# How six pairs of activations cross from FF1 to FF2: as split parts, or whole and split on arrival

## The chip, the core and the metric

The kernel runs on one NeuronCore of a Trainium2 chip. Its engines work beside each other, each with an in-order instruction stream of its own: TensorE (PE in the profile; PEld is its weight load), VectorE (DVE), ScalarE (ACT), GpSimd (POOL) and SyncE (SP), which issues most of the DMAs. The metric is the device time of one launch in microseconds, as a median of runs.

## What is computed

One inference step of a one-layer hybrid encoder, for 512 prompt tokens and 128 decode tokens, 640 in all. The change touches only the last part, the feed-forward network:

```python
def merge_and_ffn(x, oa, ob, norm_grp_a, norm_grp_b, w_out, norm_ffn, w_gate, w_up, w_down):
    o = jnp.concatenate([rmsnorm(oa, norm_grp_a), rmsnorm(ob, norm_grp_b)], axis=-1)
    x = x + o @ w_out
    h = rmsnorm(x, norm_ffn)
    return x + (jax.nn.silu(h @ w_gate) * (h @ w_up)) @ w_down
```

The model width is 2048 and the hidden width 5632, that is 44 blocks of 128, or 22 pairs of blocks. All is float32.

## The kernel before

A float32 product is made from three float32r products: each operand is split into a high part (a ScalarE copy to float32r) and a low part (the operand minus its high part, on VectorE or GpSimd). For weights this is `split` (L195, L196); `mm3` (L204 to L206) issues the three matmuls, 128x128 by 128x320.

The feed-forward network runs as 2x2 block products in Winograd's form: `quartet` (from L890) takes four weight blocks and makes seven products p1, p6, p7, p2, p5, p4, p3, which use left operands 0, 1, 2, 4, 3, 5, 6. Of the weight blocks b11, b12, b21, b22, VectorE makes b12-b22 (L927) and s6 (L929); GpSimd makes b22-s6 (L932) for p5 and b21-s6 (L941) for p4. Blocks and s6 share six tiles W, so a `w_down` load (L914, on SP) waits until an earlier block is given up, and the one into s6's tile waits for L941. The 62 tiles S hold the activations.

FF1 (the loop over `i` in NPAIR) makes one pair of hidden blocks at a time from `w_gate` and `w_up`: 8 weight tiles deep, 24 matmuls a product. Each finished pair leaves as seven left operands. `store_part` writes one of them after each later product: normally split, high part through one of two scratch tiles `half` (L992, L995) and low part (L994, L996), to `act_d`. For the pairs in `raw_pairs`, here 1, 2 and 3, the operand is written whole to `first_d` (L988).

FF2 runs 32 steps of a quartet each over `w_down`. A pair is held for eight successive steps, given by START: pairs 0 to 4 are active in step 0, pairs 1 to 5 in step 1, then five at a time until step 6. With five pairs a product has 15 matmuls. When a pair enters, `fetch` (L958, GpSimd's queue) reads its parts, 320 KB an operand; at the border `free` (called after each product of FF1's last quartet) fetches pairs 1 to 3 whole (L968), 160 KB an operand, and splits them: ScalarE L973, VectorE (pairs 1 and 3) or GpSimd (pair 2) L974. Pairs 0 and 4 come as parts. When a pair of `raw_pairs` is given up in steps 0 to 7, `after` stores its parts (L1074, SP) for its second visit. A new pair's fetch is held back by two products (`fetch_waiting`).

The order on each engine is made by a scheduler when the program is built: it places an instruction when its inputs allow, so a load or a store can stand well ahead of the code around it. Four passes add order by hand; `keep_behind` keeps marked ScalarE instructions behind the unmarked one that is written before them.

Of the kernel before, what the change touches and what calls it, by code (L numbers as in the profile page):

```python
# [41 lines left out]
def f(ap):  # L42
    return ap.bitcast(F32)
# [6 lines left out]
class Net:  # L50
# [104 lines left out]
    def keep_behind(self):  # L155

        info = mybir.DependencyInfo(mybir.DependencyClass.NoSync, mybir.DependencyReason.DATA)
        for k, block in enumerate(self.nc.cur_f.blocks):
            inside = [0] * (len(block.instructions) + 1)
            for a, b in self.behind:  # L160
                if k < len(a):
                    inside[a[k]:b[k]] = [1] * (b[k] - a[k])
            last = None
            for i, ins in enumerate(block.instructions):
                if ins.engine == mybir.EngineType.Activation:
                    if not inside[i]:
                        last = ins
                    elif last is not None:
                        self.tc.add_manual_dep(ins, last.name, info, reason="behind")

    def keep_held(self):

# [127 lines left out]
def build(nc, tc, io, pools):  # L300
# [509 lines left out]
    own_b, acts_b = group_operands(ob_d, g_b, ssq, range(8))  # L810
    n.add("decode", decode_a(1))
    x2_d, act_d = dram("x2_d", (KT, P, TOK)), dram("act_d", (7, P, NPAIR, 2, HT))
    first_d = dram("first_d", (7, P, 3, HT))
    r_a, ssq_a = n.get("S"), n.get("S")
    for m in range(KT):
        ps = n.dense([(io["w_out_b"][m], 8)], acts_b)
# [141 lines left out]
        nc.gpsimd.dma_start(out=r(sh(t, 2, HT)), in_=r(act_d[which, :, j]))  # L958
        lefts[j][which] = t, hl

    raw_pairs = active(0)[1:4]

    def free(which):
        n.put("S", *(h[which][0] for h in hs))
        for j in raw_pairs[::2]:
            k = min(2, raw_pairs[-1] + 1 - j)
            raw = n.get("S")
            dma(out=sh(raw, k, HT), in_=first_d[which, :, j - raw_pairs[0]:j - raw_pairs[0] + k])  # L968
            for a in range(k):
                t = n.get("S")  # L970
                hi, lo = hl = pack(t, HT)
                part = raw[:, a * HT:a * HT + HT]
                nc.scalar.activation(hi, part, AF.Identity)  # L973
                (nc.vector, nc.gpsimd)[a].tensor_tensor(lo, part, f(hi), ALU.subtract)  # L974
                lefts[j + a][which] = t, hl
            n.put("S", raw)
        for j in active(0):
            if j not in raw_pairs:
                fetch(j, which)

    parts = []

    def store_part():

        if parts:
            j, which, src, done = parts.pop(0)
            if j in raw_pairs:
                dma(out=first_d[which, :, j - raw_pairs[0]], in_=src)  # L988
            else:
                at = n.emitted()  # L990
                hi = n.scratch()
                nc.scalar.activation(r(hi), src, AF.Identity)  # L992
                n.behind.append((at, n.emitted()))
                nc.vector.tensor_tensor(r(src), src, hi, ALU.subtract)  # L994
                dma(out=act_d[which, :, j, 0], in_=hi)  # L995
                dma(out=act_d[which, :, j, 1], in_=src)  # L996
            n.put("S", *done)
# [62 lines left out]
    def fetch_waiting(left):  # L1060
        while len(waiting) > left:
            for j, which in waiting.pop(0):
                fetch(j, which)

    def step(t, part="all"):
        now = active(t)
# [3 lines left out]
        def after(which):  # L1070
            gone = [j for j in now if j not in nxt]
            for j in gone:
                if j in raw_pairs and t < 8:
                    dma(out=act_d[which, :, j], in_=sh(lefts[j][which][0], 2, HT))  # L1074
            n.put("S", *(lefts[j][which][0] for j in gone))
            waiting.append([(j, which) for j in nxt if j not in now])
            fetch_waiting(2)
# [11 lines left out]
        for name, bank in quartet(cnt, load, [lefts[j] for j in now], None, after, part):  # L1089
# [20 lines left out]
                add(c21, c21, bank)  # L1110
            elif name == "p3":
                add(c12, c12, bank)
            store_part()
            yield name

    def run(*args):
# [151 lines left out]
```

## Time and profile before

| | us |
|---|---|
| median of 3 runs | 2653.17 (2651.87 to 2653.21) |
| the profiled execution, its own time | 2648.2 |
| its span, first to last instruction | 2646.4 |
| PE busy | 2584.1 (98%) |
| VectorE, ScalarE, GpSimd busy | 1978.9, 1069.3, 662.1 |

PE is busy nearly throughout. Its matmuls are pipelined, so a busy PE still says little; the count of matmuls in a stretch, against the same count in a stretch without waits, tells what was lost there. FF1's last quartet runs from about 2021 us; FF2 follows it to the end. In the tables of stretches, the clock is TensorE's granted clock as a share of its full 2.4 GHz (0.50 is its lower level, 1.2 GHz), and the DMA figure is a busy share of the sixteen DMA engines.

### The profile page before, as it was taken

To read this page: it belongs to the slowest core of one execution; us is meant where nothing else is said; L and a number is where in the kernel's file an instruction comes from. 1 tells how busy PE (TensorE), PEld (TensorE's weight loads), DVE (VectorE), ACT (ScalarE), POOL (GpSimd) and SP (SyncE) were. 2 spreads that over 40 slices of the span, in tenths; PEclk is the share of its full clock that TensorE was granted. 3 is DMA by queue.
4 is the path that set the end of the run, shared out by engine and by line. 5 is a ranking of instruction groups with operands and counts; after the bars stand their busy time and mean duration, and the time that the engine had idled before them with its cause. 6 is when DMAs were issued, how large, how long until landed. Compare 5 with 4: busy or idle time off the path is not lost.

```text
span 2646.4 us, 45166 instructions
## 1 busy us (share of the span) xinstructions
PE 2584.1 (98%) x17565; PEld 2527.2 (95%) x17565; DVE 1978.9 (75%) x3071; ACT 1069.3 (40%) x1732; POOL 662.1 (25%) x577
## 2 busy tenths in 40 slices
PE   8999999999999999999999999999999799999997
PEld 8999998999899999999999999999999799999996
DVE  5665566655866888768888888888887677777797
ACT  5443344444633553333443433433444333333343
POOL 0000000000201203333333233233234432333353
PEclk9999999999999999999999999999999899999998
DMA  5322232434655433333433433433436975665655
GB/s 170 105 70 83 87 101 92 129 116 133 216 186 183 156 127 123 115 106 123 142 130 125 140 130 125 144 132 120 150 128 214 372 201 155 170 184 169 185 155 178
DMA packets 178678, 388.47 MB, mean 147 GB/s; under 512 B 21856, under 2 KB 70496, under 8 KB 178464
## 3 DMA queue, kind: packets, MB, share of 16 engines
q1 hardware_dynamic: 153120, 329.21, 38.5%
q0 software_dynamic: 24192, 55.06, 7.3%
q8 instruction: 138, 2.26, 0.4%
q10 hardware_dynamic: 1152, 1.31, 0.1%
q14 instruction: 76, 0.62, 0.1%
HBM read 301.90 MB, written 82.87 MB: 145 GB/s over the span
## 4 chain that ended last, share of the span: by engine, by line
PE 72%; DVE 5%; DMA 4%; ACT 1%; issue 1%; POOL 0%; SPq 0%; DVEq 0%; ACTq 0%
PE dn L204 15%; PE dn L206 15%; PE dn L205 14%; PE at L204 9%; PE at L206 9%; PE at L205 9%; DVE W L196 2%; DMA W<-w_down 1%; PE at L321 1%; DVE S L951 1%; DMA act_d<-half 1%; DMA S<-cka 0%; DMA S<-first_d 0%; ACT W L195 0%; PE at L402 0%
## 5 line engine op out<-in xcount | busy, mean ns | idle before, releaser
L204 PE MATMUL dn<-S,W 128*128 128x320 f32 x3694 | 1158.3, 314 | 5.0 <-ACT W L195 4.4
L206 PE MATMUL dn<-S,W 128*128 128x320 f32 x3694 | 1145.1, 310 | 12.2 <-DVE W L196 12.2
L205 PE MATMUL dn<-S,W 128*128 128x320 f32 x3694 | 1143.8, 310 | 1.1 <-DVE S L200 0.8
L195 ACT ACTIVATE W<-W 128x1024 fp32r<-128x1024 f32 (+2 forms) x632 | 608.2, 963 | 977.5 <-PE dn L205 542.5
L196 DVE TENSOR_TENSOR W<-W,W 128x1024 fp32r<-128x1024 f32 (+2 forms) x632 | 738.4, 1169 | 91.8 <-ACT W L195 88.3
L204 PEld LDWEIGHTS dn<-S,W 128*128 128x128 f32 x3694 | 695.0, 188 | 17.5 <-ACT W L195 6.1
L206 PEld LDWEIGHTS dn<-S,W 128*128 128x128 f32 x3694 | 694.4, 188 | 17.1 <-DVE W L196 15.9
L205 PEld LDWEIGHTS dn<-S,W 128*128 128x128 f32 x3694 | 694.8, 188 | 3.6 <-DVE S L200 1.0
L204 PE MATMUL at<-S,W 128*128 128x320 f32 x1594 | 494.5, 310 | 7.5 <-ACT W L195 7.5
L206 PE MATMUL at<-S,W 128*128 128x320 f32 x1594 | 495.0, 311 | 4.3 <-DVE W L196 4.3
L205 PE MATMUL at<-S,W 128*128 128x320 f32 x1594 | 493.9, 310 | 0.0
L932 POOL TENSOR_TENSOR W<-W,W 128x1024 f32<-128x1024 f32 (+2 forms) x75 | 159.4, 2126 | 641.9 <-DVE W L196 404.8
L204 PEld LDWEIGHTS at<-S,W 128*128 128x128 f32 x1594 | 300.6, 189 | 8.3 <-ACT W L195 8.3
L206 PEld LDWEIGHTS at<-S,W 128*128 128x128 f32 x1594 | 300.4, 188 | 6.5 <-DVE W L196 6.5
L205 PEld LDWEIGHTS at<-S,W 128*128 128x128 f32 x1594 | 300.5, 189 | 0.0
L951 DVE TENSOR_TENSOR S<-S,dn 128x320 f32<-128x320 f32 x358 | 163.7, 480 | 71.1 <-PE dn L206 71.0
L941 POOL TENSOR_TENSOR W<-W,W 128x1024 f32<-128x1024 f32 (+2 forms) x75 | 162.9, 2173 | 115.0 <-DVE W L196 105.1
L927 DVE TENSOR_TENSOR W<-W,W 128x1024 f32<-128x1024 f32 (+2 forms) x76 | 122.4, 1610 | 70.1 <-DMA W<-w_down 36.5
L951 DVE TENSOR_TENSOR S<-S,at 128x320 f32<-128x320 f32 x262 | 123.2, 480 | 51.4 <-PE at L206 50.5
L958 POOL DMA_DIRECT2D S<-act_d x168 | 91.7, 547 | 185.6 <-PE dn L206 94.5
L929 DVE TENSOR_TENSOR W<-W,W 128x1024 f32<-128x1024 f32 (+2 forms) x76 | 83.4, 1097 | 63.0 <-DMA W<-w_up 34.2
L994 DVE TENSOR_TENSOR S<-S,half 128x320 fp32r<-128x320 f32 x133 | 115.1, 886 | 13.5 <-ACT half L992 11.6
(153 smaller groups left out, 2125.8 us busy)
## 6 DMA issues: line engine op xcount, KB each, us to landing
S<-act_d POOLq DMA_DIRECT2D x168, 320.0 KB, 3.9
W<-w_gate SPq DMA_DIRECT2D x88, 512.0 KB
W<-w_up SPq DMA_DIRECT2D x88, 512.0 KB
W<-w_in SPq DMA_DIRECT2D x66, 512.0 KB
W<-w_down SPq DMA_DIRECT2D x64, 384.0 KB
W<-w_down SPq DMA_DIRECT2D x68, 320.0 KB
act_d<-half SPq DMA_DIRECT2D x133, 160.0 KB
act_d<-S SPq DMA_DIRECT2D x133, 160.0 KB
```

The source lines that it names most:

```text
L195: self.nc.scalar.activation(hi, src, AF.Identity)
L196: self.nc.vector.tensor_tensor(lo, src, f(hi), ALU.subtract)
L204: mm(out, a[0], b[0], start=first, stop=False)
L205: mm(out, a[0], b[1], start=False, stop=False)
L206: mm(out, a[1], b[0], start=False, stop=last)
L927: nc.vector.tensor_tensor(b12[:, w], b12[:, w], b22[:, w], sub)
L929: nc.vector.tensor_tensor(s6[:, w], b11[:, w], b12[:, w], sub)
L932: eng.tensor_tensor(b11[:, w], b22[:, w], s6[:, w], sub)
L941: eng.tensor_tensor(b21[:, w], b21[:, w], s6[:, w], sub)
L951: add = lambda o, a, b: nc.vector.tensor_tensor(o, a, b, ALU.add)
L958: nc.gpsimd.dma_start(out=r(sh(t, 2, HT)), in_=r(act_d[which, :, j]))
L994: nc.vector.tensor_tensor(r(src), src, hi, ALU.subtract)
```

## The change

`raw_pairs` becomes the six pairs 0 to 5 that are active in step 0 or 1. All are written whole in FF1. At the border `free` fetches pairs 0 to 4 whole, two at a time (0 and 1, 2 and 3, 4 alone), with VectorE splitting 0, 2 and 4 and GpSimd 1 and 3. Pair 5 is fetched whole in step 0, and pair 0 once more, whole, at the end of step 24, by the new `fetch_raw`; VectorE splits operands 0, 3 and 6 of these, GpSimd the other four. Pairs 1 to 4 (`one_store`) are stored as parts when given up. Those stores are marked, and `keep_behind` now covers SP too, so they stay behind the SP instruction written before them. `store_part` is not called in steps 0 and 1, so the last pair's parts leave from step 2 on.

```diff
--- before.py
+++ after.py
@@ -160,13 +160,14 @@
             for a, b in self.behind:
                 if k < len(a):
                     inside[a[k]:b[k]] = [1] * (b[k] - a[k])
-            last = None
-            for i, ins in enumerate(block.instructions):
-                if ins.engine == mybir.EngineType.Activation:
-                    if not inside[i]:
-                        last = ins
-                    elif last is not None:
-                        self.tc.add_manual_dep(ins, last.name, info, reason="behind")
+            for engine in (mybir.EngineType.Activation, mybir.EngineType.SP):
+                last = None
+                for i, ins in enumerate(block.instructions):
+                    if ins.engine == engine:
+                        if not inside[i]:
+                            last = ins
+                        elif last is not None:
+                            self.tc.add_manual_dep(ins, last.name, info, reason="behind")
 
     def keep_held(self):
 
@@ -810,7 +811,7 @@
     own_b, acts_b = group_operands(ob_d, g_b, ssq, range(8))
     n.add("decode", decode_a(1))
     x2_d, act_d = dram("x2_d", (KT, P, TOK)), dram("act_d", (7, P, NPAIR, 2, HT))
-    first_d = dram("first_d", (7, P, 3, HT))
+    first_d = dram("first_d", (7, P, 6, HT))
     r_a, ssq_a = n.get("S"), n.get("S")
     for m in range(KT):
         ps = n.dense([(io["w_out_b"][m], 8)], acts_b)
@@ -958,14 +959,29 @@
         nc.gpsimd.dma_start(out=r(sh(t, 2, HT)), in_=r(act_d[which, :, j]))
         lefts[j][which] = t, hl
 
-    raw_pairs = active(0)[1:4]
+    ready = active(0)
+    raw_pairs = active(0) + [j for j in active(1) if j not in ready]
+    one_store = raw_pairs[1:5]
+
+    def fetch_raw(j, which, engine):
+        t, spare = n.get("S"), None
+        if len(n.lists["S"]) > 3:
+            spare = n.get("S")
+        raw = n.scratch() if spare is None else spare[:, :HT]
+        dma(out=raw, in_=first_d[which, :, j])
+        hi, lo = hl = pack(t, HT)
+        nc.scalar.activation(hi, raw, AF.Identity)
+        engine.tensor_tensor(lo, raw, f(hi), ALU.subtract)
+        if spare is not None:
+            n.put("S", spare)
+        lefts[j][which] = t, hl
 
     def free(which):
         n.put("S", *(h[which][0] for h in hs))
-        for j in raw_pairs[::2]:
-            k = min(2, raw_pairs[-1] + 1 - j)
+        for j in ready[::2]:
+            k = min(2, ready[-1] + 1 - j)
             raw = n.get("S")
-            dma(out=sh(raw, k, HT), in_=first_d[which, :, j - raw_pairs[0]:j - raw_pairs[0] + k])
+            dma(out=sh(raw, k, HT), in_=first_d[which, :, j:j + k])
             for a in range(k):
                 t = n.get("S")
                 hi, lo = hl = pack(t, HT)
@@ -974,9 +990,6 @@
                 (nc.vector, nc.gpsimd)[a].tensor_tensor(lo, part, f(hi), ALU.subtract)
                 lefts[j + a][which] = t, hl
             n.put("S", raw)
-        for j in active(0):
-            if j not in raw_pairs:
-                fetch(j, which)
 
     parts = []
 
@@ -985,7 +998,7 @@
         if parts:
             j, which, src, done = parts.pop(0)
             if j in raw_pairs:
-                dma(out=first_d[which, :, j - raw_pairs[0]], in_=src)
+                dma(out=first_d[which, :, j], in_=src)
             else:
                 at = n.emitted()
                 hi = n.scratch()
@@ -1060,7 +1073,10 @@
     def fetch_waiting(left):
         while len(waiting) > left:
             for j, which in waiting.pop(0):
-                fetch(j, which)
+                if j in raw_pairs and j not in one_store:
+                    fetch_raw(j, which, nc.vector if which % 3 == 0 else nc.gpsimd)
+                else:
+                    fetch(j, which)
 
     def step(t, part="all"):
         now = active(t)
@@ -1070,8 +1086,10 @@
         def after(which):
             gone = [j for j in now if j not in nxt]
             for j in gone:
-                if j in raw_pairs and t < 8:
+                if j in one_store and t < 8:
+                    at = n.emitted()
                     dma(out=act_d[which, :, j], in_=sh(lefts[j][which][0], 2, HT))
+                    n.behind.append((at, n.emitted()))
             n.put("S", *(lefts[j][which][0] for j in gone))
             waiting.append([(j, which) for j in nxt if j not in now])
             fetch_waiting(2)
@@ -1110,7 +1128,8 @@
                 add(c21, c21, bank)
             elif name == "p3":
                 add(c12, c12, bank)
-            store_part()
+            if t > 1:
+                store_part()
             yield name
 
     def run(*args):
```

GpSimd at the end of FF1, around b21-s6 of the last quartet (L941, then L942). In the names, S and W are tiles, with a number of the tile and one of its use. Before:

```order
L974 TENSOR_TENSOR S27_3184_21531<-S32_3182_21526,S27_3184_21531 128x320
L958 DMA S40_3187_21539<-act_d_7841 128x640
L1040 TENSOR_TENSOR S8_3152_21296<-S8_3152_21296,S36_1948_11142 128x640
L958 DMA S2_3188_21541<-act_d_7841 128x640
L958 DMA S57_3196_21586<-act_d_7841 128x640
L958 DMA S44_3197_21588<-act_d_7841 128x640
L958 DMA S32_3208_21636<-act_d_7841 128x640
L974 TENSOR_TENSOR S48_3193_21578<-S28_3191_21573,S48_3193_21578 128x320
L941 TENSOR_TENSOR W11_3209_21639<-W11_3209_21639,W1_3179_21496 128x1024
L958 DMA S28_3207_21634<-act_d_7841 128x640
L958 DMA S36_3360_22458<-act_d_7841 128x640
L974 TENSOR_TENSOR S39_3204_21626<-S50_3202_21621,S39_3204_21626 128x320
```

After:

```order
L990 TENSOR_TENSOR S27_3163_21447<-S32_3161_21442,S27_3163_21447 128x320
L1053 TENSOR_TENSOR S8_3131_21212<-S8_3131_21212,S36_1948_11142 128x640
L959 DMA S36_3326_22273<-act_d_7841 128x640
L990 TENSOR_TENSOR S40_3166_21455<-S10_3164_21450,S40_3166_21455 128x320
L942 TENSOR_TENSOR W11_3191_21567<-W11_3191_21567,W1_3158_21412 128x1024
L990 TENSOR_TENSOR S32_3173_21498<-S41_3171_21493,S32_3173_21498 128x320
L990 TENSOR_TENSOR S45_3185_21550<-S12_3183_21545,S45_3185_21550 128x320
L990 TENSOR_TENSOR S57_3176_21506<-S10_3174_21501,S57_3176_21506 128x320
L990 TENSOR_TENSOR S10_3188_21558<-S43_3186_21553,S10_3188_21558 128x320
L990 TENSOR_TENSOR S15_3197_21603<-S23_3195_21598,S15_3197_21603 128x320
L990 TENSOR_TENSOR S37_3200_21611<-S1_3198_21606,S37_3200_21611 128x320
L990 TENSOR_TENSOR S20_3210_21662<-S18_3208_21657,S20_3210_21662 128x320
```

Six fetches of parts are gone from this stretch, and two GpSimd splits of operand 0 now stand ahead of b21-s6, where one of operand 0 and one of operand 1 stood.

SP's queue at the border, from the first split pair up to the `w_down` load into s6's tile (W1). Before:

```order
L1074 DMA act_d_7841<-S51_3183_21528 128x640
L968 DMA S10_3185_21534<-first_d_7842 128x320
L968 DMA S32_3194_21581<-first_d_7842 128x320
L1074 DMA act_d_7841<-S27_3184_21531 128x640
L968 DMA S28_3191_21573<-first_d_7842 128x640
L914 DMA W10_3255_21849<-w_down 128x640
L1074 DMA act_d_7841<-S3_3186_21536 128x640
L968 DMA S50_3202_21621<-first_d_7842 128x640
L968 DMA S45_3205_21629<-first_d_7842 128x320
L968 DMA S34_3213_21670<-first_d_7842 128x640
L914 DMA W1_3256_21851<-w_down 128x640
```

After:

```order
L984 DMA S10_3164_21450<-first_d_7842 128x640
L984 DMA S2_3167_21458<-first_d_7842 128x320
L915 DMA W10_3241_21793<-w_down 128x640
...
L984 DMA S23_3195_21598<-first_d_7842 128x640
L984 DMA S1_3198_21606<-first_d_7842 128x640
L984 DMA S24_3201_21614<-first_d_7842 128x320
L984 DMA S18_3208_21657<-first_d_7842 128x640
L915 DMA W1_3242_21795<-w_down 128x640
```

The three stores of parts (L1074) between the fetches are gone, and the `w_down` load stands behind more fetches.

SP's queue after that. Before, from the load of step 1's b11 (W0) on; W11 is its b21, W10 the first block of step 2, and `half`, S17 and S4 are the last pair's parts:

```order
L914 DMA W0_3293_22056<-w_down 128x640
L995 DMA act_d_7841<-half_3274_21962 128x320
L914 DMA W11_3304_22129<-w_down 128x640
L996 DMA act_d_7841<-S17_3141_21226 128x320
L995 DMA act_d_7841<-half_3278_21991 128x320
L996 DMA act_d_7841<-S4_3198_21590 128x320
L995 DMA act_d_7841<-half_3283_22019 128x320
L914 DMA W10_3320_22222<-w_down 128x640
```

After, from the load of step 2's b11 (W1) on; W11 is its b21, W6, W10 and W0 belong to step 3, and `half` and S8 are the last pair's parts:

```order
L915 DMA W1_3309_22161<-w_down 128x640
L1091 DMA act_d_7841<-S27_3163_21447 128x640
L915 DMA W11_3322_22250<-w_down 128x640
L1091 DMA act_d_7841<-S15_3197_21603 128x640
L915 DMA W6_3344_22369<-w_down 128x640
L915 DMA W10_3345_22371<-w_down 128x640
L1008 DMA act_d_7841<-half_3313_22188 128x320
L1008 DMA act_d_7841<-half_3316_22215 128x320
L915 DMA W0_3346_22373<-w_down 128x640
L1009 DMA act_d_7841<-S8_3131_21212 128x320
L1091 DMA act_d_7841<-S32_3173_21498 128x640
```

The parts stood between the loads of steps 1 and 2; now the first of them that `store_part` writes within FF2 come after all four loads of step 2 and two of step 3, and the stores of the pairs given up (L1091) begin here.

## Rows read from the trace of the kernel before

**Rows 1.** Stretches: us; PE, PEld, DVE, ACT, POOL busy (count); clock; DMA; GB/s.
```profile
1200.00:1900.00 700.00, 700.00 (x4775) 700.00 (x4774) 589.29 (x639) 277.07 (x354) 227.63 (x114) 1.00 0.40 132
2030.00:2040.00 10.00, 9.35 (x62) 8.82 (x61) 6.71 (x9) 3.70 (x8) 8.28 (x9) 1.00 1.07 361
2040.00:2050.00 10.00, 6.12 (x26) 5.36 (x26) 5.59 (x9) 4.34 (x8) 5.40 (x9) 0.83 1.09 368
2050.00:2070.00 20.00, 15.42 (x97) 14.23 (x97) 15.54 (x23) 7.37 (x15) 15.34 (x20) 1.00 1.12 391
2070.00:2090.00 20.00, 12.30 (x50) 10.78 (x50) 10.58 (x18) 5.53 (x10) 5.51 (x8) 0.66 1.13 389
2090.00:2120.00 30.00, 28.24 (x191) 27.71 (x190) 21.17 (x35) 9.87 (x15) 8.14 (x10) 1.00 1.02 343
2120.00:2160.00 40.00, 40.00 (x275) 40.00 (x274) 30.70 (x48) 14.30 (x21) 13.03 (x14) 1.00 0.61 172
2440.00:2520.00 80.00, 80.00 (x547) 80.00 (x547) 62.00 (x93) 27.58 (x35) 29.84 (x34) 1.00 0.65 183
```

**Rows 2.** What PE waited for, 2020 to 2120 us: total, times, longest.
```profile
PE at L204 <- ACT W L195: 7.0, 2, 5.0
PE dn L206 <- DVE W L196: 6.6, 8, 1.5
```

**Rows 3.** Chain that ended last, 2021 to 2100 us: start, us, what.
```profile
2028.00 4.51 DMA S<-first_d
...
2034.98 3.39 POOL W L941
...
2038.38 3.39 DMA W<-w_down
...
2048.43 7.02 DMA S<-first_d
...
2059.30 0.32 SPq L995
...
2067.74 11.63 DMA act_d<-half
...
2086.71 0.74 DVE W L196
```

**Rows 4.** ScalarE in time, 2060 to 2085 us: start, us, line, idle before.
```profile
2073.91 0.47 ACT L992 ACTIVATE half<-S 128x320 fp32r<-128x320 f32 x1 [7.34 <-DMA act_d<-half]
```

**Rows 5.** SP's queue in time, 2063 to 2076 us.
```profile
2075.35 0.41 SPq L914 DMA_DIRECT2D W<-w_down  x1
```

**Rows 6.** DMA queues (share at the end) and issues, 2020 to 2120 us.
```profile
q1 hardware_dynamic: 10846, 21.24, 61.2%
q0 software_dynamic: 5596, 12.74, 38.8%
...
S<-act_d POOLq DMA_DIRECT2D x39, 320.0 KB, 6.9
act_d<-S SPq DMA_DIRECT2D x21, 320.0 KB
```

**Rows 7.** PE in time, 2021 to 2070 us: first matmuls of p4 and of step 0.
```profile
2041.67 0.42 PE L204 MATMUL at<-S,W 128*128 128x320 f32 x1 [2.04 <-ACT W L195]
...
2053.73 0.38 PE L204 MATMUL dn<-S,W 128*128 128x320 f32 x1
```

**Rows 8.** The present splits, line 974: count, min/median/max ns.
```profile
L974 DVE TENSOR_TENSOR S<-S,S x14: 477/493/1860, 2021.3 to 2056.0; 128x320 fp32r<-128x320 f32 x14
L974 POOL TENSOR_TENSOR S<-S,S x7: 862/1094/1556, 2025.6 to 2053.6; 128x320 fp32r<-128x320 f32 x7
```

**Rows 9.** GpSimd by line, 2020 to 2120 us: busy, mean ns, idle before.
```profile
L958 POOL DMA_DIRECT2D S<-act_d x39 | 21.4, 555 | 19.4 <-DVE W L927 8.4 <-PE dn L206 4.3 <-PE at L206 3.2
...
L941 POOL TENSOR_TENSOR W<-W,W 128x640 f32<-128x640 f32 (+1 forms) x4 | 8.4, 2094 | 3.5 <-DVE W L196 3.5
```

**Rows 10.** VectorE by line, 2013 to 2115 us: busy, mean ns, idle before.
```profile
L974 DVE TENSOR_TENSOR S<-S,S 128x320 fp32r<-128x320 f32 x14 | 10.4, 743 | 12.2 <-ACT S L973 12.2
```

## The prediction

> **What bounds the kernel now.** I read the stretches first. From 1200 to 1900 us PE is busy for 700.00 of 700 us and issues 4775 matmuls, 0.1466 us each [rows 1]. I use that pace as the measure everywhere: a stretch loses its length minus its matmuls at 0.1466 us. From 2030 us on:
>
> - 2030 to 2040: 62 matmuls are 9.1 us, 0.9 lost.
> - 2040 to 2050: 26 are 3.8, 6.2 lost.
> - 2050 to 2070: 97 are 14.2, 5.8 lost.
> - 2070 to 2090: 50 are 7.3, 12.7 lost.
> - 2090 to 2120: 191 are 28.0, 2.0 lost.
> - 2120 to 2160: 275 are 40.3, nothing lost [rows 1].
>
> The border from FF1 to FF2 thus loses 27.6 us. That is all a change made here can win, 1.0% of the execution. In these stretches the DMA engines move 343 to 391 GB/s with a busy share about 1.1, against 132 GB/s and 0.40 in FF1 [rows 1].
>
> The waits of PE show what comes last: the split of a weight block, on ScalarE (7.0 us in two waits) or VectorE (6.6 us in eight) [rows 2]. The weight blocks are behind something else, and the chain names it in three places [rows 3]. First, a fetch of raw pairs lands after 4.51 us, and GpSimd's b21-s6 (L941), queued behind the split of that pair, runs only at 2034.98, for 3.39 us. The `w_down` load that waits for its tile goes out at 2038.38 and takes another 3.39. Second, a raw fetch issued at 2048.43 needs 7.02 us. Third, the store of one `half` needs 11.63 us from 2067.74. There are two such scratch tiles, so ScalarE stood 7.34 us, until 2073.91, before it could fill the next [rows 4]; SP, in order, stood with the store of that fill, and issued the load of step 1's b11 behind it only at 2075.35 [rows 5]. This third place is the 12.7 us.
>
> **The change part by part.** *FF1.* Pairs 0, 4 and 5 lose 21 splits and half of their bytes in stores. PE there has no wait at all (700.00 of 700), with VectorE busy for 589.29 [rows 1]. Worth 0; the change only takes work away from there.
>
> *Bytes at the border.* 39 fetches of 320 KB and 21 stores of 320 KB are issued there between 2020 and 2120 us [rows 6]. Of the fetches, 21 (pairs 0, 4, 5, seven operands each) become 160 KB: 3.4 MB less. The 21 stores, 6.9 MB, move behind the loads of step 2 (the two orders of SP show it), as do six of the last pair's parts, twelve stores of 160 KB, 2.0 MB. What FF1's last products and steps 0 and 1 must have by the end of step 1 is 42 raw operands (6.9 MB), eight `w_down` blocks (2.6 MB) and four tiles of x2 (1.3 MB): 10.8 MB, 28 us at 389 GB/s. From 2022 to the end of step 1 there would be 24 us of FF1 and 2 times 105 matmuls (30.8 us), 55 us. So the engines are no longer full there, and landings near 4.5 us rather than 7.0 are what I take [rows 3].
>
> *FF1's last quartet.* b21-s6 stands on GpSimd behind two splits of operand 0, of which the second waits for a raw fetch of which SP issues the first part before any store. The operand-1 split that held it until 2034.98 is now behind it. Operand 0 is given up one product (24 matmuls, 3.5 us) before operand 1, so b21-s6 should start near 2031.5 and end near 2034.9, where it ended at 2038.37. p4 began at 2041.67 after a wait of 2.04 us [rows 7], so it is due at 2039.6; a weight split of 1.4 still fits, and a fetch of 7.0 (2.5 later) too. The 6.2 us go to 0. The 0.9 lost before that stays at half, 0.5.
>
> *GpSimd and VectorE at the border.* GpSimd: 18 splits (14 at the border, 4 for pair 5) instead of 7, so 11 more at 1.09 us [rows 8], 12.0 us; 21 fetches fewer at 0.555 [rows 9], 11.7 us. Even. VectorE: 24 splits instead of 14, 10 more at 0.49 [rows 8], 4.9 us, and six pairs of part subtractions gone to step 2; it was busy for 6.71 of 10, 5.59 of 10, 15.54 of 20 us [rows 1]. ScalarE: 42 copies instead of 21, 21 more at the 0.47 of a copy of the same shape [rows 4], 9.9 us, in stretches where it was busy for less than half [rows 1]. All this is hidden unless one of them stands in front of a weight split; that is the next term and the last rival.
>
> *Step 0.* Here something new comes last. b21-s6 of step 0 (before p4) stands on GpSimd behind pair 5's splits. These wait on SP behind a part store of FF1's last pair, which can go once that operand is made: at step 0's start, 2053.73 [rows 7], at the earliest, and as late as the first such store now, 2059.30 [rows 3], 5.6 later. I take the middle, 2.8. Then one landing, 4.5 [rows 3], a copy, 0.5, three splits at 1.1 [rows 8], one fetch issue, 0.6, one addition (L1051, priced like a split, 1.1), and the small b21-s6, 1.7 (8.4 less the large one's 3.4, by three) [rows 9], then a weight split, 0.7 for the copy and 0.7 for the subtraction [rows 3]: 15.9 us. p4 is due after five products of 15 matmuls, 11.0 us. 4.9 lost, 2.1 to 7.7 by the ends, in place of 5.8.
>
> *Step 1.* Its b11 is issued once that b21-s6 is done; until it is needed there are p4 and p3 (4.4 us) and p4's split (1.4), against a landing of 4.5 and a split. 0.5 lost, up to 3.3 with a landing of 7.0. The 12.7 us go with the part stores.
>
> *Steps 2 to 6, where the stores go.* Five steps are 525 matmuls, 77 us. In them fall 28 stores (21 and pair 4's seven; 9.2 MB), the part stores (2.0), `w_down` (6.6), the fetches of pairs 6 to 9 (9.2) and x2 (3.3): 30 MB, or 26 MB if pair 6 and three steps of x2 come early, as their place in the order allows. That is 338 to 393 GB/s. The nearest row is 2090 to 2120 with 343 GB/s: 2.0 us lost in 30 [rows 1], so 5.1 in 77. On top comes the chain over the two `half` tiles, between 0 and the 12.7 us it cost before. It is nearest to 0 because step 2's four loads and two of step 3 stand ahead of it; I take 1.5.
>
> The Trainium skill (DMA: Bandwidth & Descriptors, "Issuing engines are not separate DMA queues") says that DMAs issued from any engine run on the same 16 DMA engines and interleave, so moving fetches from GpSimd's queue to SP's wins no transfer time. The trace agrees: both queues' shares add up to 100% [rows 6]. Its table (section "Specifications") puts HBM at about 358 GB/s for a core; the 391 GB/s above are more, and the measurement decides. By the page, 30 MB would need 84 us, 7 more than those steps have: an estimate, 1.9 us worse than my 5.1.
>
> *Step 24.* Pair 0 comes back whole: four GpSimd splits at 1.09 for seven fetches at 0.555, ScalarE 3.3 us, VectorE 1.5 [rows 4, 8], in a stretch where PE is busy for 80.00 of 80 us and GpSimd for 29.84 [rows 1]. 0, at most one late landing of about 2.5 us.
>
> *Sum.* Before 27.6; after 0.5 + 0 + 4.9 + 0.5 + 5.1 + 1.5 = 12.5. Gain 15.1: the profiled execution of 2648.2 would be 2633.1. That execution is 5.0 below the median, so the median comes to 2638.1.
>
> **The rivals.** *A, this sum:* 2638, with 2631 to 2647 by the terms' ends. *B, cleaner than that:* step 0's chain starts with its store ready at once, and stores behind the loads cost nothing: 0.5 + 2.1 + 0.5 + 1 remain, gain 23.5, 2630. For it: at 172 GB/s, 2120 to 2160, nothing was lost [rows 1]. Against: steps 2 to 6 carry twice that. *C, displaced:* the two `half` tiles meet 28 stores in steps 2 and 3, and the wait of 12.7 us returns there in full, beside the 12.5 without its 1.5: 23.7 remain, gain 3.9, 2649; with seven stores delaying one more load by 4 us, 2653. For it: the store of a `half` took 11.63 us [rows 3] exactly when stores filled the engines, and the same two tiles and the same SP queue stand there. It decides when such a store takes above 8 us. This also is the change doing half of what it says.
>
> *D, slower:* VectorE and GpSimd hold each other up. A VectorE split took 477 ns at least and 493 in the median, but 1860 once, and a GpSimd one 862 to 1556 [rows 8]. If all 24 of VectorE's took 1.86 us they would need 44.6 us instead of the 10.4 of the fourteen now (mean 743 ns) [rows 10], 34 more. VectorE's idle time between 2030 and 2070 us is 12.2 [rows 1] and the part subtractions that left are 6; 16 us of late weight splits stay. Such waits halve the clock: 10 us at 0.83 and 20 at 0.66 [rows 1] are 8.5 us given away. 12.5 + 16 + 8.5 = 37.0 remain, 9.4 more than before: 2663. It decides when the mean VectorE split is above 1.4 us. Against it: the median is at the floor.
>
> The Trainium skill (SBUF — State Buffer, "SBUF: two separate sides") has the rule behind D: a VectorE op with two SBUF inputs and a GpSimd op lock the shared port pair for the whole instruction, whichever starts first. By that, more splits on both engines wait for each other. The trace has the long cases (1860 against 477 ns) but only few of them.
>
> **How the numbers follow.** A 0.55, B 0.17, C 0.19, D 0.09. About 0.2%, 5.3 us, is what a measurement of this kernel can tell from no change, so faster ends at 2647.9 and slower begins at 2658.5. A and B are faster, and so is about a third of C (a shorter return of the wait): 0.78. The rest of C is the same: 0.13. D is slower: 0.09. The range must reach A, B and most of C: 2627 to 2651. Below 2627 almost the whole loss would be gone; above 2651 lie the top of C, and D.
>
> **What would show it.** Right: 2040 to 2050 us full of matmuls; the DMA rate below 380 GB/s until the end of step 1; b21-s6 of FF1's last quartet ending by 2035; a wait of some 5 us before p4 of step 0; no wait for a `half` near a `w_down` load in step 1; small waits in steps 2 to 6 at the rate of 2090 to 2120. Wrong: raw fetches still landing after 7 us, waits above 4 us in step 2 or 3 with `half` in the chain (C), VectorE splits above 1.4 us on average (D), or a granted clock below 0.9 anywhere after 2050.

## The result: 0.25% slower, where 0.5% faster was forecast

The changed kernel takes 2657.59 us in the median (2654.8 to 2661.35, 12 runs), the kernel before 2651.78 (12 runs): a ratio of 1.0025, 95% interval 1.0016 to 1.0034. The profiled execution has a span of 2653.1 us against 2646.4, 6.7 us more. By the count of matmuls, about 4 us less than before are lost in it from 2020 to 2080 us, 8 more from 2080 to 2200 and 1.2 more from 2400 to 2600; another 1.3 lie before 1000 us, where both kernels run the same code.

Stretches of the changed kernel, columns as in [rows 1], whose last seven rows they answer:

```profile
2030.00:2040.00 10.00, 7.05 (x49) 6.79 (x47) 10.00 (x8) 4.54 (x11) 6.69 (x6) 1.00 0.66 213
2040.00:2050.00 10.00, 9.50 (x54) 9.48 (x55) 10.00 (x13) 7.43 (x17) 6.93 (x6) 0.83 0.89 294
2050.00:2070.00 20.00, 12.22 (x66) 11.50 (x65) 20.00 (x27) 9.38 (x22) 14.27 (x14) 0.83 0.71 237
2070.00:2090.00 20.00, 17.99 (x119) 17.26 (x119) 13.20 (x19) 6.73 (x11) 10.79 (x13) 1.00 0.96 325
2090.00:2120.00 30.00, 25.51 (x164) 25.25 (x163) 23.32 (x40) 10.62 (x18) 4.76 (x5) 0.94 0.60 190
2120.00:2160.00 40.00, 35.56 (x232) 35.10 (x231) 25.46 (x39) 12.28 (x19) 14.40 (x17) 0.96 1.00 351
2440.00:2520.00 80.00, 78.71 (x537) 78.48 (x536) 61.09 (x89) 29.03 (x40) 30.62 (x31) 1.00 0.54 151
```

The bytes left the border as forecast: 213 to 294 GB/s up to 2070 us, where it had been 361 to 391. But the third busy time, VectorE's, is 10.00 of 10, 10.00 of 10 and 20.00 of 20 from 2030 to 2070. It was 27.84 of these 40 us before [rows 1]. VectorE has become the engine that PE waits for most. (These busy times include time in which a VectorE instruction stands and is held up, as the rows below show.)

The same view cut at the steps: FF1's last quartet, step 0, step 1, and from there to 2200 us.

```profile
2022.40:2054.60 32.20, 26.74 (x170) 26.20 (x169) 32.01 (x33) 21.52 (x45) 21.62 (x16) 0.95 0.67 219
2054.60:2079.00 24.40, 18.28 (x105) 17.56 (x105) 22.51 (x31) 8.26 (x18) 17.51 (x19) 0.86 0.69 224
2079.00:2102.90 23.90, 17.75 (x105) 17.02 (x106) 14.70 (x23) 6.03 (x10) 5.89 (x6) 0.93 0.76 260
2102.90:2200.00 97.10, 91.52 (x612) 90.79 (x611) 69.89 (x112) 34.67 (x53) 30.01 (x34) 0.98 0.86 288
```

At 0.1466 us a matmul the four lose 7.3, 9.0, 8.5 and 7.4 us, 32.2 in all. What PE waited for from 2020 to 2120 us (total, times, longest), where [rows 2] had stood, begins with VectorE:

```profile
PE dn L207 <- DVE W L197: 8.9, 3, 4.5
PE dn L205 <- DVE S L952: 8.1, 3, 4.8
PE dn L205 <- ACT W L196: 0.7, 1, 0.7
```

VectorE by line, same stretch (count, then busy, mean ns, idle before):

```profile
L197 DVE TENSOR_TENSOR W<-W,W 128x640 fp32r<-128x640 f32 (+1 forms) x30 | 31.3, 1048 | 1.7 <-ACT W L196 1.6
L990 DVE TENSOR_TENSOR S<-S,S 128x320 fp32r<-128x320 f32 x21 | 21.2, 1040 | 3.4 <-ACT S L989 3.4
L952 DVE TENSOR_TENSOR S<-S,dn 128x320 f32<-128x320 f32 x20 | 9.2, 477 | 0.8 <-PE dn L207 0.8
```

The same 21 splits in the form of [rows 8], with the shortest, the median and the longest:

```profile
L990 DVE TENSOR_TENSOR S<-S,S x21: 476/1143/4504, 2022.5 to 2060.6; 128x320 fp32r<-128x320 f32 x21
```

L990 is the split of the border (L974 before; in the new kernel L974 is pair 5's split). It takes 1040 ns in the mean, where the prediction counted 490. L952, an addition of the same shape that reads one operand from PSUM (TensorE's result banks), keeps its 477. The time goes where both operands lie in SBUF (the memory that holds the tiles). What that looks like in time: VectorE (start, us, line), and GpSimd beside it.

```profile
2031.80 4.91 DVE L990 TENSOR_TENSOR S<-S,S 128x320 fp32r<-128x320 f32 x2
```

```profile
2031.85 0.90 POOL L990 TENSOR_TENSOR S<-S,S 128x320 fp32r<-128x320 f32 x1
2032.69 2.42 POOL L942 TENSOR_TENSOR W<-W,W 128x1024 f32<-128x1024 f32 x1
2035.07 0.88 POOL L990 TENSOR_TENSOR S<-S,S 128x320 fp32r<-128x320 f32 x1
```

Two VectorE splits end only at 2036.7, after three GpSimd instructions in a row have ended at 2035.95.

### The profile page after: what moved, and what is told of

It is laid out like the page before. It is cut to its first block, busy times and chain, and to the rows that moved or that the text cites. A ratio compares the mean times of both kernels' runs of the same rounds, so it can differ in the third digit from the quotient of the medians.

```text
span 2653.1 us, 45127 instructions
## 1 busy us (share of the span) xinstructions
PE 2586.3 (97%) x17565; PEld 2531.2 (95%) x17565; DVE 1979.1 (75%) x3063; ACT 1071.5 (40%) x1739; POOL 664.5 (25%) x564
## 4 chain that ended last, share of the span: by engine, by line
PE 70%; DVE 6%; DMA 4%; ACT 1%; issue 1%; SPq 0%; POOL 0%; DVEq 0%; ACTq 0%; POOLq 0%
PE dn L205 14%; PE dn L207 14%; PE dn L206 14%; PE at L205 9%; PE at L206 8%; PE at L207 8%; DVE W L197 2%; DMA W<-w_down 2%; DVE S L952 1%; PE at L322 1%; DMA S<-first_d 1%; ACT W L196 0%; PE at L403 0%; DMA W<-w_gate 0%; DVE S L990 0%
## 5 line engine op out<-in xcount | busy, mean ns | idle before, releaser
L197 DVE TENSOR_TENSOR W<-W,W 128x1024 fp32r<-128x1024 f32 (+2 forms) x632 | 734.7, 1163 | 104.9 <-ACT W L196 101.4
L952 DVE TENSOR_TENSOR S<-S,dn 128x320 f32<-128x320 f32 x358 | 163.6, 480 | 76.5 <-PE dn L207 75.8
L942 POOL TENSOR_TENSOR W<-W,W 128x1024 f32<-128x1024 f32 (+2 forms) x75 | 161.9, 2159 | 123.9 <-DVE W L197 113.1
L928 DVE TENSOR_TENSOR W<-W,W 128x1024 f32<-128x1024 f32 (+2 forms) x76 | 132.4, 1742 | 70.6 <-DMA W<-w_down 37.1
L952 DVE TENSOR_TENSOR S<-S,at 128x320 f32<-128x320 f32 x262 | 123.2, 480 | 55.8 <-PE at L207 55.3
L930 DVE TENSOR_TENSOR W<-W,W 128x1024 f32<-128x1024 f32 (+2 forms) x76 | 84.1, 1106 | 62.8 <-DMA W<-w_up 32.2
L959 POOL DMA_DIRECT2D S<-act_d x140 | 76.4, 547 | 167.0 <-PE dn L207 80.1
L1007 DVE TENSOR_TENSOR S<-S,half 128x320 fp32r<-128x320 f32 x112 | 97.4, 892 | 2.2 <-ACT half L1005 0.6
```

The source lines that it names most:

```text
L197: self.nc.vector.tensor_tensor(lo, src, f(hi), ALU.subtract)
L928: nc.vector.tensor_tensor(b12[:, w], b12[:, w], b22[:, w], sub)
L930: nc.vector.tensor_tensor(s6[:, w], b11[:, w], b12[:, w], sub)
L942: eng.tensor_tensor(b21[:, w], b21[:, w], s6[:, w], sub)
L952: add = lambda o, a, b: nc.vector.tensor_tensor(o, a, b, ALU.add)
```

## Experiments

In all of them the loss is the stretch's length less its matmuls at 0.1466 us, from 2020 to 2080 and from 2080 to 2200 us. (The first two expectations have 20.7 and 6.1 for the kernel before and 13.8 after 2080 for the changed one; they added up shorter stretches, of which each hides about 0.3 us.) Ratios are to the kernel before on the same chip, where its median was 2649.3 to 2651.3. Each loss is read from one traced execution, which lay up to 4 us from its kernel's median (e8's 3.9 below it), so a difference of one or two microseconds between two losses is not shown.

| kernel | median us | ratio, 95% interval | lost to 2080 | lost after |
|---|---|---|---|---|
| before | 2651.8 | 1 | 20.9 | 7.1 |
| the change | 2657.6 | 1.0025, 1.0016 to 1.0034 | 17.0 | 15.2 |
| e1_whole_only | 2651.2 | 0.9999, 0.9990 to 1.0009 | 18.5 | 7.9 |
| e2_stores_only | 2647.1 | 0.9988, 0.9979 to 0.9998 | 18.2 | 7.9 |
| e3_dve_all | 2649.3 | 0.9996, 0.9986 to 1.0005 | 15.3 | 9.3 |
| e4_pool_all | 2663.9 | 1.0049, 1.0034 to 1.0064 | 24.4 | 14.2 |
| e5_parts_early | 2652.3 | 1.0009, 1.0000 to 1.0018 | 18.8 | 12.0 |
| e6_no_behind | 2652.2 | 1.0012, 1.0003 to 1.0021 | 16.0 | 13.3 |
| e7_dve_poolq | 2648.2 | 0.9993, 0.9983 to 1.0002 | 15.3 | 10.3 |
| e8_dve_parts4 | 2648.4 | 0.9995, 0.9985 to 1.0004 | 14.3 | 7.4 |
| e9_parts4 | 2656.2 | 1.0019, 1.0010 to 1.0029 | 17.8 | 12.0 |
| e10_dve_p5 | 2645.8 | 0.9981, 0.9972 to 0.9990 | 12.8 | 9.6 |
| e11_old_parts4 | 2645.2 | 0.9979, 0.9970 to 0.9989 | 17.6 | 4.9 |
| e12_old_parts4_dve | 2643.0 | 0.9972, 0.9962 to 0.9981 | 15.0 | 6.7 |
| e13_p5_dve | 2655.4 | 1.0017, 1.0007 to 1.0026 | 15.4 | 15.2 |
| e14_old_parts7_dve | 2639.5 | 0.9963, 0.9950 to 0.9976 | 15.6 | 3.3 |
| e15_dve_p5_parts7 | 2644.0 | 0.9974, 0.9964 to 0.9984 | 13.1 | 5.2 |

### Which half of the change costs: e1, e2

The changed kernel without its moves of stores:

```diff
-                    at = n.emitted()
                     dma(out=act_d[which, :, j], in_=sh(lefts[j][which][0], 2, HT))
-                    n.behind.append((at, n.emitted()))
-            if t > 1:
-                store_part()
+            store_part()
```

> The changed kernel with both moves of stores taken back: the pairs' stores are not marked and the last pair's parts leave in steps 0 and 1 again; all six pairs are still fetched whole and split. The changed kernel loses 17.0 us of PE's pace from 2020 to 2080 us and 13.8 from 2080 to 2200, 30.8 in all (before: 20.7 and 6.1). Theory S (the 35 splits themselves cost it, VectorE being held while GpSimd computes): the loss up to 2080 stays at 17 or grows to 20 to 25 with the stores back in it, and the median is 2657 to 2668. Rival D (what was gained is given back by the stores moved behind step 1): the loss after 2080 falls to about 4, the median is near 2650.

The other half alone, put into the kernel before:

```diff
+                    at = n.emitted()
                     dma(out=act_d[which, :, j], in_=sh(lefts[j][which][0], 2, HT))
+                    n.behind.append((at, n.emitted()))
-            store_part()
+            if t > 1:
+                store_part()
```

(with `keep_behind` over SP as in the change).

> The kernel before with only the stores moved: the stores of pairs 1 to 3 are marked and kept behind on SP, and the last pair's parts leave from step 2 on; fetches and splits as before. Theory S (splits cost it): the loss from 2020 to 2080 falls from 20.7 to under 10, after 2080 it is at most 13.8, and the median is 2640 to 2649. Rival D (the moved stores give it back): the loss after 2080 is 13 to 14 as in the changed kernel, up to 2080 about 15, the median about 2654.

Neither theory takes both. The whole fetches alone (e1) are worth nothing (0.9999): the loss up to 2080 is 18.5 us, near S's, but the median is where D had it, 6 us below S's range, and the loss after 2080 is 7.9, not D's 4. The moved stores alone (e2) gain a little (0.9988): the median is in S's range, but 18.2 us stay lost up to 2080, where S wanted less than 10. Neither half loses against the kernel before. Only together do they, and all of it after 2080 (15.2 us, where each half has 7.9).

### Who holds VectorE: e3, e4

```diff
-                (nc.vector, nc.gpsimd)[a].tensor_tensor(lo, part, f(hi), ALU.subtract)
+                nc.vector.tensor_tensor(lo, part, f(hi), ALU.subtract)
```

> The changed kernel with all 35 border splits on VectorE and none on GpSimd. Theory S (in the changed kernel a VectorE split takes 1.04 us in the mean instead of 0.49, because GpSimd's splits run at the same time): the mean falls below 0.65 us, the loss from 2020 to 2080 from 17.0 to below 11, the median to about 2651. Rival Q (the splits stand in VectorE's queue behind late landings and copies, and the weight splits behind them, whoever else computes): the mean stays near 1.0, the loss up to 2080 rises to 19 or more, the median to 2660 or more.

VectorE now makes 35 splits in less time than the 21 of the changed kernel took. Its splits by line, 2020 to 2070 us:

```profile
L990 DVE TENSOR_TENSOR S<-S,S 128x320 fp32r<-128x320 f32 x35 | 17.1, 546 | 4.0 <-ACT S L989 4.0
```

The mean is 546 ns, as S said, and the median came down by 8 us to 2649.3. The loss up to 2080 fell less than S wanted (to 15.3, not below 11); most of the gain lies after it. Pair 5's splits are still shared here, and five weight splits of 128x640 took 1709 ns each in the mean between 2030 and 2070 us (1005 in the changed kernel, 1106 in e10 below, where pair 5 is VectorE's too).

In e4 the line has `nc.gpsimd` for both.

> The changed kernel with all 35 border splits on GpSimd and none on VectorE. Theory S (GpSimd's work holds VectorE's): VectorE's weight splits in 2020 to 2070 us get longer than their 1.05 us mean, b21-s6 comes late behind 38 us of splits, the loss up to 2080 is above 20, the median above 2662. Rival Q (VectorE's order is the matter): without splits in its queue VectorE is in time, the loss up to 2080 is below 12, the median about 2652.

S again, but for a reason sharper than a longer mean: one VectorE instruction. VectorE, then GpSimd, then PE in time:

```profile
2034.05 23.88 DVE L928 TENSOR_TENSOR W<-W,W 128x640 f32<-128x640 f32 x1 [0.55 <-DMA W<-w_down]
```

```profile
2033.47 2.56 POOL L990 TENSOR_TENSOR S<-S,S 128x320 fp32r<-128x320 f32 x3
2036.00 2.41 POOL L942 TENSOR_TENSOR W<-W,W 128x1024 f32<-128x1024 f32 x1
2038.37 18.87 POOL L990 TENSOR_TENSOR S<-S,S 128x320 fp32r<-128x320 f32 x23
```

```profile
2059.51 0.63 PE L207 MATMUL dn<-S,W 128*128 128x320 f32 x1 [20.17 <-DVE W L197]
```

A subtraction that takes some 0.8 us (816 ns in the mean of the changed kernel) stood 23.88, until GpSimd's unbroken row of 27 instructions ended at 2057.24. PE waited 20.17 us for the weight split queued behind it. The weight splits that S named are no longer than in the changed kernel (1550 ns for the large ones, 1556 there).

### Which of the moved stores: e5, e6

e5 is the changed kernel with `store_part()` in every step, e6 the one without the two `behind` lines; each is half of e1's edit.

> The changed kernel with one of its two moves of stores taken back: the last pair's parts leave in steps 0 and 1 again; the pairs' stores stay marked. The changed kernel loses 17.0 us from 2020 to 2080 us and 15.2 from 2080 to 2200. Theory C (in step 2 the part stores, which wait for the two half tiles, stand on SP with the pairs' stores ahead of a w_down load): without them the loss after 2080 falls below 9, up to 2080 it is 17 to 20, the median 2650 to 2653. Rival W (the bytes of the pairs' stores in steps 2 and 3 are too many, whatever their order): the loss after 2080 stays above 12, the median 2656 or more.

> The changed kernel with the other move taken back: the pairs' stores are not marked and stand where the scheduler places them, the last pair's parts leave from step 2 on. Theory C (parts and pairs' stores together stand ahead of a w_down load in step 2): with the pairs' stores gone from there the wait at 2120 us shrinks to under 3, the loss after 2080 to about 9, up to 2080 it grows from 17 to 19 or more, the median about 2653. Rival P (the chain of part stores over the two half tiles is enough by itself): the loss after 2080 stays above 12, the median at 2658 or more.

Both medians lie within 3 us of the one forecast by C, but not by its steps: 12.0 and 13.3 us stay lost after 2080. Neither store alone makes up the loss there. 7.8 and 6.8 us of it lie from 2080 to 2100, where the changed kernel loses 7.5; the next run looks there.

### Step 1: e13

e13 changes, in the changed kernel, `nc.vector if which % 3 == 0 else nc.gpsimd` to `nc.vector` in `fetch_waiting`.

> The changed kernel with only pair 5's and the returning pair 0's splits moved to VectorE; the border's 35 splits stay shared. Theory G (in the changed kernel the fetches of parts stand on GpSimd behind pair 5's splits, go out in one burst from 2072 us and make the w_down load of 8.90 us late, 6.0 us lost between 2090 and 2100): that loss falls below 2, the loss after 2080 from 15.2 to 10 or less, the median from 2657.6 to about 2652. Rival V (the load is late because VectorE, held by the border's splits, gives its tile up late): the loss between 2080 and 2100 stays at 5 or more, the median at 2656 or more.

G fell: the loss after 2080 stayed at 15.2. V's loss held, and the median, 2655.4, is just under V's. 2080 to 2100 us in the changed kernel, below it in e13, and last in e3:

```profile
2080.00:2100.00 20.00, 14.70 (x85) 13.94 (x86) 11.71 (x19) 4.29 (x7) 3.64 (x3) 0.91 0.79 275
```

```profile
2080.00:2100.00 20.00, 15.17 (x91) 14.94 (x92) 11.05 (x20) 4.31 (x8) 3.14 (x2) 0.91 0.69 232
```

```profile
2080.00:2100.00 20.00, 20.00 (x137) 19.80 (x137) 15.56 (x25) 8.34 (x14) 4.73 (x3) 1.00 0.58 177
```

7.5 and 6.7 us lost. e3, which differs from the changed kernel only in the border's splits, loses nothing from 2080 to 2100.

### The stores in steps 2 to 4: e7, e8, e9

On e3's splits, e7 issues the part stores from GpSimd's queue, and e8 puts `if t > 3` in place of `if t > 1`; e9 has e8's edit on the changed kernel itself.

> The changed kernel with all border splits on VectorE (2649.3 us, loss 15.3 up to 2080 and 9.3 after), and the last pair's part stores in FF2 issued from GpSimd's queue instead of SP's; bytes and steps as they are. Theory C (SP's order): the wait of some 7 us between 2110 and 2130 falls below 2, the loss after 2080 below 4, the median to 2643. Rival W (too many bytes in step 2): the wait stays above 5, the median at 2648 or more.

C fell. No part store stood ahead of a w_down load on SP any more, and 6.5 us stayed lost from 2110 to 2130 (92 matmuls). Two links of e7's chain there:

```profile
2106.04 4.79 DMA act_d<-half
...
2116.46 7.25 DMA W<-w_down
```

The `half` still holds ScalarE's next copy, VectorE's L1007 stands in order behind that copy, and the load takes 7.25 us at 374 GB/s (6.73 in e3). But the part stores now stand in GpSimd's order, among its fetches and subtractions, so e7 does not test what no order at all would give.

> The changed kernel with all border splits on VectorE, and the last pair's parts stored from step 4 on instead of step 2. Theory C (order on SP): no wait above 2 us in step 2, where the pairs' stores are alone; where the parts meet other pairs' stores in step 4, a wait of up to 7 us may come back there: median 2643 to 2649. Rival W (bytes of the pairs' stores): the wait of some 7 us near 2120 us stays, the median at 2648 or more.

> The changed kernel, its border splits as they are, with the last pair's parts stored from step 4 on instead of step 2. Theory H (the chain over the two half tiles together with the pairs' stores costs the 5.8 us near 2120 us): the loss after 2080 falls from 15.2 to 10 or less, up to 2080 it stays at 17, the median is about 2652. Rival M (it only moves to step 4): the loss after 2080 stays at 14 or more, with a wait between 2140 and 2180, the median 2656 or more.

2110 to 2130 us in e3, and below it in e8:

```profile
2110.00:2130.00 20.00, 14.80 (x85) 14.54 (x84) 8.75 (x16) 3.73 (x7) 7.46 (x10) 0.83 1.08 392
2110.00:2130.00 20.00, 18.98 (x129) 18.71 (x128) 14.65 (x22) 7.59 (x13) 6.36 (x6) 1.00 0.75 230
```

With the parts two steps later, the loss there goes from 7.5 us to 1.1, and some 4 come back between 2150 and 2170; e8's median is in C's range, but equal to e3's within the intervals. In e9 2120 to 2130 improves from 4.6 to 1.2, but the median by no more than its interval: step 1's loss is still there, and 3.5 us are lost from 2140 to 2180. M had that wait and that median, though not its loss of 14; H had neither a loss of 10 nor a median of 2652.

### Both causes taken away: e10, e11, e12, e14, e15

e10 is e8 with pair 5 and pair 0 split on VectorE too (e13's edit).

> All border splits on VectorE and the parts from step 4 on (2648.4 us, loss 14.3 up to 2080), and now pair 5's and the returning pair 0's splits on VectorE too. Theory S (GpSimd's splits hold VectorE: an addition in step 0, L1061, of a shape that takes 0.48, took 3.23 us there): that addition falls below 0.6 us, the loss from 2050 to 2070 from 6.4 to below 4, the median to 2646. Rival F (VectorE is simply full there, 10.00 of 10 us, and eight more splits make it worse): the loss up to 2080 stays at 14 or grows, the median at 2648 or more.

S had the addition and the median right; from 2050 to 2070 the loss fell only from 6.7 to 4.9, and more is lost after 2080 (9.6 us against 7.4). The addition L1061 by line from 2020 to 2080 us, in e8 and in e10:

```profile
L1061 DVE TENSOR_TENSOR S<-S,S 128x320 f32<-128x320 f32 x1 | 3.2, 3226 | 0.0
```

```profile
L1061 DVE TENSOR_TENSOR S<-S,S 128x320 f32<-128x320 f32 x1 | 0.5, 477 | 0.0
```

e11 is e2 with `if t > 3`; e12 adds e3's edit, for its 21 splits; e14 is e12 with `if t > 6`; e15 is e10 with `if t > 6`.

> The kernel before with the pairs' stores marked and the last pair's parts from step 4 on; fetches and splits as before. With the parts from step 2 on (2647.1 us) it lost 18.2 us up to 2080 and 7.9 after, 7.2 of them between 2120 and 2130. Theory H (parts and half chain): these 7.2 fall below 2, the loss after 2080 to about 3, the median to 2642. Rival M (moved to step 4, or the pairs' stores alone are enough): the loss after 2080 stays at 6 or more, the median at 2646 or more.

> The same, with all three whole pairs split on VectorE (21 splits, GpSimd none). Theory S (GpSimd's splits hold VectorE): the mean split falls from 0.87 us to below 0.65, the loss up to 2080 from 18.2 to 16 or less, the median to 2640. Rival F (the fetches of parts and whole pairs come late anyway): the loss up to 2080 stays at 18, the median at that of the run without this edit.

e11's 7.2 us fell to 1.1, but the loss after 2080 only to 4.9, between H and M. In e12 the mean split is what S forecast, and the loss up to 2080 fell to 15.0; its median is 2 us below e11's, with intervals that overlap:

```profile
L975 DVE TENSOR_TENSOR S<-S,S 128x320 fp32r<-128x320 f32 x21 | 11.0, 550 | 10.6 <-ACT S L974 10.6
```

> The kernel before with its three whole pairs split on VectorE, the pairs' stores marked, and the last pair's parts from step 7 on, when no pair is stored any more (from step 4 on: 2643.0 us, loss 6.7 after 2080). Theory H (parts and pairs' stores must not meet): the loss from 2140 to 2180 goes to 0 and no new one appears near 2210, the median is 2641. Rival M (the parts cost the same wherever they go): the loss reappears near step 7, between 2190 and 2230, the median stays at 2643.

> The changed kernel with all splits on VectorE, pair 5's too, and the last pair's parts from step 7 on (from step 4 on: 2645.8 us, 9.6 lost after 2080, 7.3 of them from 2160 to 2180). Theory H: these 7.3 fall to below 1 and nothing comes back near step 7; the median is about 2640, equal to the kernel with three whole pairs and the same stores. Rival W (28 pairs' stores instead of 21 fill steps 2 to 4 by themselves): 5 or more stay lost between 2140 and 2180, the median 2645.

e14 is the best kernel of the study, 2639.5 us, 0.37% below the one before: three pairs whole, all split on VectorE, the pairs' stores kept behind, the last pair's parts once no pair is stored any more. Its two stretches:

```profile
2020.00:2080.00 60.00, 48.10 (x303) 45.74 (x302) 46.48 (x66) 24.26 (x43) 32.82 (x42) 0.97 0.97 325
2080.00:2200.00 120.00, 117.37 (x796) 116.61 (x796) 91.02 (x142) 43.90 (x66) 38.54 (x42) 1.00 0.82 259
```

H's signs came in e14: nothing is lost from 2140 to 2180, and 0.3 us from 2190 to 2230. e15 shows what six pairs instead of three are worth with both causes taken away: nothing. By the traces 2.5 us less are lost up to 2080, 1.9 more after it (1.6 of its loss from 2140 to 2180, where H wanted less than 1 and W 5 or more), and some 2 more from 2400 to 2600 (10.2 against 8.2). H's "equal" was not met: 2644.0 is 4 us above e14, and ten runs of 2641.2 to 2649.0 stand against six of 2637.2 to 2643.6, though the intervals of the ratios overlap.

## Why the prediction was wrong

**The bytes, right.** The rate fell, the raw fetches on the chain up to 2060 us took 3.63 to 5.40 us, with none of 7.02, and b21-s6 of FF1's last quartet ended at 2035.11 (2032.69 and 2.42 above), where 2034.9 was forecast.

```profile
2030.76 5.40 DMA S<-first_d
...
2040.22 4.64 DMA S<-first_d
...
2050.20 3.63 DMA S<-first_d
```

**"GpSimd and VectorE at the border", the step that failed.** It priced ten more VectorE splits at the 0.49 of the median of [rows 8], 4.9 us, and called them hidden. [Rows 10] had the mean, 743 ns, beside it. Measured: 21 border splits take 21.2 us, where fourteen took 10.4 (the other three of the 24 are pair 5's). More than the price, the cover was wrong. VectorE's idle time before was idle waiting for transfers, over ScalarE's copies of what had landed; in the kernel before, 2013 to 2115 us:

```profile
L973 ACT ACTIVATE S<-S 128x320 fp32r<-128x320 f32 x21 | 9.2, 464 | 21.7 <-DMA S<-first_d 14.6 <-DMA act_d<-S 5.7 <-DVE S L974 1.4
```

With the transfers early there was none left, 40.00 of 40 us, of which some 10 are VectorE held up (21 splits at e3's 546 ns are 11.5 us, not 21.2). Weight splits, in order behind the splits of activations, came late. e3 shows that GpSimd's share of the splits makes them slow, not their number, and that the sharing is worth 8 us of the median.

**FF1's last quartet**, forecast at 0.5, lost 7.3. b21-s6 was in time; what came last instead was VectorE: PE's longest wait there, 3.45 us until 2040.50, is for L197. PE's longest waits in this quartet and in step 0:

```profile
2040.50 0.64 PE L207 MATMUL dn<-S,W 128*128 128x320 f32 x1 [3.45 <-DVE W L197]
...
2063.06 0.60 PE L205 MATMUL dn<-S,W 128*128 128x320 f32 x1 [4.78 <-DVE S L952]
```

**Step 0**, forecast at 4.9 in front of p4, lost 9.0, and elsewhere: 4.8 us of it before p6, for a VectorE addition (L952) behind two held splits. From 2063 to 2068 us, right after that wait, the granted clock was 0.52 and PE issued 19 matmuls, where full pace has 34: another 2.2 us. The chain that the forecast followed, over pair 5's splits to b21-s6, was not what came last.

**Step 1**, forecast at 0.5, lost 8.5. The chain:

```profile
2072.97 4.92 DMA S<-first_d
...
2083.98 8.90 DMA W<-w_down
...
2113.87 2.66 DMA act_d<-half
...
2120.27 0.68 SPq L1091
...
2121.50 1.07 SPq L1091
2122.61 6.26 DMA W<-w_down
```

The w_down load in its second row went out late, after VectorE's split had given its tile up at 2083.97, and needed 8.90 us; PE waited 4.49 for it. Ahead of that split, in VectorE's order, stood one of pair 5's, whose fetch is the first row. By e3, which treats pair 5 as the change does and loses nothing here, it takes the border's shared splits to make this late; by e13, pair 5's splits on GpSimd are not needed for it. How the lateness passes from the border to this load was not followed.

**Steps 2 to 6**, forecast at 6.6 with the `half` chain, lost 7.4 up to 2200. That the size agrees is luck: it was to be many small waits, and 4.6 us of it lie from 2120 to 2130, most of them in one wait.

```profile
2129.68 0.63 PE L205 MATMUL at<-S,W 128*128 128x320 f32 x1 [4.44 <-ACT W L196]
```

Rival C's mechanism is there in part, a `half` in the chain and stores (L1091) and parts ahead of the load at 2122.61, though that `half` took 2.66 us and not more than 8. e7 speaks against the order on SP as the reason; e8 and e14 show that parts and pairs' stores must not fall together. Whether they cost through the two `half` tiles or through their bytes was not separated.

**Step 24**, forecast at 0, lost 1.3 (537 matmuls in 80 us instead of 547). The kernels with three whole pairs don't have it, but neither has e4, which fetches pair 0 whole, so its cause is open.

**The rivals.** What happened is D's mechanism, to which 0.09 was given, with its price wrong both ways: it was to decide from a mean of 1.4 us, and decided at 1.04; it was to end at 2663, and ended at 2657.6. Of the other signs of being wrong, two came: a granted clock of 0.83 from 2050 to 2070 us, and C's wait above 4 us in step 2 or 3. The reason written against it, that the median is at the floor, was the mistake: a median doesn't show that a few splits carry all the delay, and the change put more work of both engines side by side, which is what makes such cases.

The Trainium skill (SBUF — State Buffer, "SBUF: two separate sides") says that a VectorE instruction with two SBUF inputs and a GpSimd one that reads SBUF exclude each other for a whole instruction. The runs agree: L990 at 1040 ns with GpSimd splitting, 546 without; L952, with one input in PSUM, at 477 beside it. It also says that the one that starts first gets the ports; e4's subtraction of 23.88 us shows that the engine that waits need not be next when that instruction ends.

**Open.** 13 to 16 us stay lost up to 2080 us in the best kernels; which part of it is VectorE's order and which the landings was not separated. So the two causes don't account for the whole miss: the sum left 12.5 us, the change lost 32.2 up to 2200, and e15, with both causes taken away, still loses 18.3.

## What to carry to other kernels

Work that is split over VectorE and GpSimd to halve it can take longer than on VectorE alone, when both read two operands from SBUF: price it by the mean beside a busy GpSimd, not by a median from a stretch where the two rarely met, and look which instructions stand behind it. An engine's idle time is cover only as long as what it idles for stays late: a change that brings the data early takes the cover away. Stores that are moved out of one crowded stretch need a stretch where no others go.

## What the runs showed of the hardware

A VectorE subtraction of two SBUF operands that takes about 0.8 us lasted 23.88 us while GpSimd ran 27 tensor instructions without a gap, and ended 0.7 us after the last of them. A row of short GpSimd instructions can thus hold VectorE for all its length; one run shows it at that length, and in the changed kernel a split of 476 ns at least lasted 4504 ns beside three GpSimd instructions. ScalarE's copies (452 to 474 ns in the run with the 23.88) and VectorE's additions out of PSUM (470 to 490 ns in the changed kernel) showed nothing of the kind.
